# Hybrid diffusion step: the merge takes over h's buffers and runs beside the last gate projections, the MLP's first part stays in the merge's PSUM set, and the modulation sums are spread anew

## The chip, the cores and the metric

The kernel runs on one core of a Trainium2 chip. The metric is device time in microseconds (us) of one execution, as a median over runs. The profile is one execution, taken by the hardware profiler.

## The reference

Two token sets (512 noisy latent tokens, 128 context tokens, so T = 640 rows of width 1024) go through two layers with the same weights. Cut to what matters here:

```python
mod = silu(c) @ w_mod[l] + b_mod[l]                  # 6 vectors of 1024, for c and for c_ctx
sh1, sc1, g1, sh2, sc2, g2 = split(mod, 6)           # vectors 0, 1, 2, 3, 4, 5
h = rmsnorm(x, g_pre_mix) * (1 + sc1) + sh1
z = h @ w_in                                         # q, k, v of mixers A, B, C and 3072 gate columns
oa, ob, oc = three attention mixers
m = (sigmoid(ga) * (oa @ w_oa) + sigmoid(gb) * (ob @ w_ob) + sigmoid(gc) * (oc @ w_oc))
x = x + g1 * rmsnorm(m @ w_out, g_post_mix)
h = rmsnorm(x, g_pre_mlp) * (1 + sc2) + sh2
x = x + g2 * rmsnorm(square(relu(h @ w_mlp1)) @ w_mlp2, g_post_mlp)
```

Everything is float32. The kernel forms each product from high and low halves of its operands, three matmuls per tile.

## The kernel before

The Python code does not issue instructions at once. It records them with the tiles that they read and write, and a list scheduler (`Recorder`) then puts all of them into one order per engine. In that order TensorE (PE) takes ready work by its place in the recorded program, and the other engines by how late an operation may be. A tile pool that opens at the place of a closed one lets no instruction of its own be placed before the last instruction of the closed one has been. All DMAs are issued by SP, in order, so one that waits holds back those behind it. Since one function issues every recorded operation, the profile names line 526 for all of them, and rows are told apart by tile names.

A layer l runs through these stages (times of layer 0, of layer 1 in brackets):

- Mixer B (to 280 us; to 1480 us): projections, `b_rope`, then eight heads.
- Mixers A and C (280 to 607 us; 1480 to 1762 us), called AC below. Attention is a chain over PE, ScalarE (ACT), VectorE (DVE) and GpSimd (POOL): products into `sps`, softmax into `pt`, transposes into `tps`, products into `ops`.
- Fillers run beside both. `gate_gen` computes the 24 gate blocks in 48 half steps (24 matmuls into `gps`, a tanh on ACT, a DMA of `th` to DRAM) and needs h, which lives in `hh` and `hl`. `mod_gen` computes the modulation vectors. One vector has two halves, and each half has four steps that load 512 KB of `w_mod` and add them into `macc0` on DVE and `macc1` on POOL (7 additions per half), and one step with small matmuls into `mps`. The rates say how many filler steps go with a step of attention. Inside attention `mod_gen` loads into `wr`, a ring of three buffers that all weights share.
- The merge (617 to 700 us; 1782 to 1870 us): `merge` loads the mixers' outputs back from DRAM (12 loads `orw`), splits them into `oh` and `ol`, and multiplies into `sps`, in the order of mixers 1 (B), 0 (A), 2 (C); the gates come back as `tg`. The result m goes to `mh` and `ml`.
- `wout` (products `fps`, then norm and transposes `nps`), then `mlp1_first`, the first 512 columns of the MLP in two parts: 384 tokens, then 256.
- `up` (the rest of the MLP's first product) and `down` (`mlp2_block`), with modulation sums as fillers that have a ring `mr` of their own.

Before the change, gates and sums end first, then the pools of the fillers and of h close, and the merge's pools open in their place. PSUM has eight banks. The merge and `wout` use the set big=2 (two tiles of two banks), pt=2, o=1, fill=1, and `mlp1_first` opens the set ring=6, pt=2.

Of the kernel before, what the change touches and what calls it, by code (L numbers as in the profile page):

```python
# [11 lines left out]
F32 = mybir.dt.float32  # L12
F32R = mybir.dt.float32r
# [4 lines left out]
P = 128  # L18
D = 1024
KC = 8  # L20
DEPTH = 2
NT = 5
T = 640
# [11 lines left out]
GATE_RATE_B = 0.03  # L35
MOD_RATE = 0.2
GATES_FIRST = 2
# [9 lines left out]
ACT_BUFS = 10  # L47
UP_RATE = (0.7, 0.5)
DOWN_RATE = (1.6, 0.5)

# [479 lines left out]
class Step:  # L530
# [1380 lines left out]
    def run(self):  # L1911
        nc, tc, I, O = self.nc, self.tc, self.I, self.O
        with ExitStack() as ctx:
# [14 lines left out]
            self.hh = hp.tile([P, KC, T], F32R, name="hh")  # L1928
            self.hl = hp.tile([P, KC, T], F32R, name="hl")
            with pool("n0") as np_:  # L1930
                self.first_norm(np_, xin)
# [4 lines left out]
            for l in range(DEPTH):  # L1936
                self.fine = False
                stack2 = ExitStack()
                fpool = stack2.enter_context(pool(f"fill{l}", "right"))
                mods = [self.mod_gen(fpool, 0, (2, 3, 4, 5))] if l == 0 else []  # L1940
                gl = [self.gate_gen(fpool, l)]
                fills = gl + mods

                with pool(f"b{l}") as bp:
# [13 lines left out]
                    with pool(f"bh{l}") as bh, self.banks(f"psb{l}", big=2, ring=4, alias={"pt": "ring", "fill": "ring", "o": "ring"}):  # L1958
                        self.NP = P_BUFS_B
                        hs = self.b_heads(bh, l)  # L1960
                        self.drive(hs[0][0], (fills, 1))
                        self.drive(self.zip(hs[0][1], hs[1][0]), (gl, GATE_RATE_B), (mods, MOD_RATE))
                        for h in range(8):
                            steps = [hs[h][2]]
                            if h < 7:
                                steps.append(hs[h + 1][1])
                            if h < 6:
                                steps.append(hs[h + 2][0])
                            self.drive(self.zip(*steps), (gl, GATE_RATE_B if h < 7 else 1), (mods, MOD_RATE))

                self.fine = True
                with pool(f"ac{l}") as ap, self.banks(f"psac{l}", big=2, ring=3, o=1, alias={"pt": "ring", "fill": "ring"}):
# [17 lines left out]
                    self.finish(*gl, *mods)  # L1990
                stack2.close()
                stack.close()
                pstack = ExitStack()
                pstack.enter_context(self.banks(f"ps{l + 1}", big=2, pt=2, o=1, fill=1))

                stack = ExitStack()
                with pool(f"mm{l}", sides[l % 2]) as mmp, pool(f"wx{l}", sides[l % 2]) as wx:
                    mh = mmp.tile([P, KC, T], F32R, name="mh")
                    ml = mmp.tile([P, KC, T], F32R, name="ml")
                    us = {}  # L2000
# [4 lines left out]

                    with pool(f"m{l}") as mp:
                        mg = self.merge(mp, l, mh, ml)
                        self.finish(itertools.islice(mg, 33))
                        load(0, wx)
                        self.finish(mg)  # L2010
                    hside = sides[1 - l % 2]
                    hp = stack.enter_context(pool(f"h2{l}", hside))
                    self.h2h = hp.tile([P, KC, T], F32R, name="h2h")
                    self.h2l = hp.tile([P, KC, T], F32R, name="h2l")
                    hstack = ExitStack()
                    self.hfull = hstack.enter_context(pool(f"hf{l}", hside)).tile([P, KC, T], F32, name="hfull")
                    with pool(f"w{l}") as wp:
# [23 lines left out]
                with pool(f"up{l}", side) as mp:  # L2041
                    t = self.sums(mp)
                    self.finish(self.mlp1_first(mp, "r", 3, l, us, slice(FIRST_TOKENS, T)))
                    self.hfull = None
                    hstack.close()
                    modp = hstack.enter_context(pool(f"md{l}", hside))
                    mods = [self.mod_gen(modp, 1, (5,), 2)] if last else [self.mod_gen(modp, l + 1, range(5), 2)]
                    kept = {"pool": kstack.enter_context(pool(f"kept{l}", hside))}
                    halfs = self.halfs()

                    def up():
                        for n in range(4, 32, 2):
                            self.mlp1_pair(mp, l, n, t, halfs, kept if n >= 32 - KEPT else None)
                            yield

                    self.drive(up(), (mods, UP_RATE[l]))
                with pool(f"dn{l}", side) as mp:
# [13 lines left out]
                    with pool(f"end{l}", hside) as ep:  # L2071
# [14 lines left out]
                hstack.close()  # L2086
                self.hh, self.hl = self.h2h, self.h2l
# [62 lines left out]
```

## Time and profile before

| | before |
|---|---|
| runs | 2389.28, 2395.51, 2398.93 us (median 2395.51) |
| profiled execution | 2388.71 us |
| its span, first to last instruction | 2386.9 us |
| PE busy | 2296.2 us (96%) |
| DVE busy | 1703.2 us (71%) |
| ACT busy | 1294.2 us (54%) |
| POOL busy | 767.6 us (32%) |
| mean granted PE clock | 0.988 |

The span is shorter than the execution by 1.8 us, which lie before the first and after the last instruction. A granted clock of 1.00 is 2.4 GHz and 0.50 is 1.2 GHz. In a stretch with a mean clock of 0.79, a share of 0.21 of the stretch is lost as against the full clock.

### The profile page before, as it was taken

The numbers are of one execution on the slowest core, as the hardware profiler recorded it, in microseconds if no ns is written. First come the engines' busy times: TensorE is split into PE (matmuls) and PEld (weight loads), VectorE is DVE, ScalarE is ACT, GpSimd is POOL, SyncE is SP. The second block draws the span as 40 slices with busy tenths as digits, with TensorE's granted clock in tenths as the row PEclk, the third lists the DMA queues.
The fourth block names the chain that finished last, engine by engine and source line by source line (L and its number), as shares of the span: only waits on it lengthen the run. The fifth ranks groups of instructions, "written<-read, shape, count | busy, mean of one in ns | idle before, by whom it ended". The sixth has DMA issues, their size and how long they took to land. (4 is left out here: it accounts for less than half of the span.)

```text
span 2386.9 us, 39558 instructions
## 1 busy us (share of the span) xinstructions
PE 2296.2 (96%) x14303; PEld 2101.0 (88%) x14303; DVE 1703.2 (71%) x3347; ACT 1294.2 (54%) x2996; POOL 767.6 (32%) x671
## 2 busy tenths in 40 slices
PE   8998999999899899999999999999989999999998
PEld 3987999989898899987889989999989988998886
DVE  3689678797574899888865684776756659895444
ACT  4578566666334566654444674655653355664222
POOL 1346233452132366334421121233312315650001
PEclk9999999999899999999999999999999999999999
DMA  7443423333563454576534323222236543546432
GB/s 248 117 141 99 141 76 100 102 108 104 179 198 117 147 164 156 172 239 218 175 111 106 74 65 92 64 63 77 74 101 199 172 135 132 172 140 208 129 116 82
DMA packets 252451, 317.10 MB, mean 133 GB/s; under 512 B 37328, under 2 KB 169696, under 8 KB 251744
## 3 DMA queue, kind: packets, MB, share of 16 engines
q1 hardware_dynamic: 252256, 314.58, 42.0%
q8 instruction: 113, 1.85, 0.3%
q14 instruction: 82, 0.67, 0.1%
HBM read 251.84 MB, written 57.44 MB: 130 GB/s over the span
## 5 line engine op out<-in xcount | busy, mean ns | idle before, releaser
L526 DVE TENSOR_TENSOR wl<-wr,wh 128x256 fp32r<-128x256 f32 (+5 forms) x768 | 380.4, 543 | 151.5 <-ACT wh L526 147.0
L526 ACT ACTIVATE wh<-wr 128x256 fp32r<-128x256 f32 (+5 forms) x768 | 276.1, 421 | 206.0 <-PE lps L526 122.5
L526 POOL TENSOR_SCALAR pt<-pt,rc 128x640 f32<-128x640 f32 (+1 forms) x192 | 168.8, 887 | 361.9 <-DVE rc L526 310.4
L526 PE MATMUL lps<-wh,ah 128*128 128x512 f32 x640 | 254.1, 397 | 0.0
L526 PE MATMUL lps<-wl,ah 128*128 128x512 f32 x640 | 253.1, 395 | 0.0
L526 PE MATMUL lps<-wh,al 128*128 128x512 f32 x640 | 253.0, 395 | 0.0
L526 POOL TENSOR_TENSOR rs<-ss,mhalf 128x1 f32<-128x1 f32 x60 | 38.2, 637 | 453.9 <-DVE ss L526 453.7
L526 POOL TENSOR_TENSOR macc<-macc,mr 128x512 f32<-128x512 f32 x84 | 126.2, 1503 | 171.8 <-ACT mr L526 155.5
L526 DVE TENSOR_TENSOR pl<-tps,ph 128x512 fp32r<-128x512 f32 (+2 forms) x240 | 147.5, 630 | 32.5 <-ACT ph L526 30.2
L526 ACT ACTIVATE pt<-sps,nm 128x640 f32<-128x640 f32 (+2 forms) x192 | 141.7, 740 | 44.6 <-DVE nm L526 38.8
L526 PE MATMUL sps<-h2h,wl 128*128 128x320 f32 (+2 forms) x464 | 145.3, 313 | 12.1 <-DVE wl L526 12.1
L526 PE MATMUL sps<-h2h,wh 128*128 128x320 f32 (+2 forms) x464 | 145.7, 314 | 6.2 <-DVE f L526 6.2
L526 ACT ACTIVATE ph<-tps 128x512 fp32r<-128x512 f32 (+2 forms) x240 | 129.6, 555 | 30.2 <-PE tps L526 26.7
L526 PEld LDWEIGHTS lps<-wl,ah 128*128 128x128 f32 x640 | 120.7, 189 | 28.4 <-issue 0.7
L526 PEld LDWEIGHTS lps<-wh,ah 128*128 128x128 f32 x640 | 120.7, 189 | 28.0 <-issue 0.5
L526 PEld LDWEIGHTS lps<-wh,al 128*128 128x128 f32 x640 | 120.6, 188 | 27.6 <-issue 0.2
L526 PE MATMUL sps<-h2l,wh 128*128 128x320 f32 (+2 forms) x464 | 144.7, 312 | 0.0
L526 PE MATMUL tps<-ident,pt 128*128 128x128 f32 x896 | 140.3, 275 | 4.1 <-POOL pt L526 3.0
L526 PE MATMUL sps<-oh,wh 128*128 128x320 f32 x384 | 122.1, 321 | 16.2 <-ACT oh L526 16.2
L526 POOL TENSOR_TENSOR s<-wq 128x512 f32<-128x512 f32 x56 | 90.2, 1611 | 134.6 <-DMA wq<-in_w_mlp 102.3
L526 DVE TENSOR_TENSOR wl<-s,wh 128x512 fp32r<-128x512 f32 x112 | 129.0, 1165 | 4.0 <-ACT wh L526 3.9
L526 PE MATMUL sps<-ol,wh 128*128 128x320 f32 x384 | 122.8, 321 | 0.0
(335 smaller groups left out, 7341.7 us busy)
## 6 DMA issues: line engine op xcount, KB each, us to landing
wr<-in_w_in SPq DMA_DIRECT2D x72, 512.0 KB, 3.8
wr<-in_w_mlp SPq DMA_DIRECT2D x72, 512.0 KB, 4.1
wq<-in_w_mlp SPq DMA_DIRECT2D x56, 512.0 KB, 4.7
mr<-in_w_mod SPq DMA_DIRECT2D x48, 512.0 KB, 4.5
ar<-a SPq DMA_DIRECT2D x56, 320.0 KB, 4.9
wr<-in_w_mod SPq DMA_DIRECT2D x32, 512.0 KB, 3.7
th<-th SPq DMA_DIRECT2D x96, 160.0 KB, 2.0
tg<-th SPq DMA_DIRECT2D x48, 320.0 KB, 3.0
```

Source lines behind the costliest of these rows:

```text
L526: getattr(getattr(self.nc, o.eng), o.name)(*args, **kw)
```

## The change

- Layer l's last four gate steps (`GATES_LAST`) are taken out of attention's list and driven beside the first steps of `merge`. For that the filler pool and h's pool stay open, and `mh` and `ml` take the ring places of `hh` and `hl` (for layer 1 of `h2h` and `h2l`) instead of a pool of their own. Layer 1's filler pool moves to the left side.
- The merge's PSUM set becomes big=2, pt=2, fill=2, and stays open through the first part of `mlp1_first`.
- The vectors' sums move: before, layer 0's attention computes vectors 2 to 5 of layer 0, layer 0's MLP vectors 0 to 4 of layer 1, and layer 1's MLP vector 5 of layer 1. Now attention of each layer computes that layer's vectors 2 to 4 with rate 0 in mixer B's heads and 0.3 in AC, layer 0's MLP computes vector 5 of layer 0 and vectors 0 and 1 of layer 1, and layer 1's MLP vector 5 as before. The MLP's rates fall from 0.7 and 1.6 to 0.5 and 1.0.

```diff
-MOD_RATE = 0.2
+MOD_RATE = 0.3
+MOD_RATE_B = 0.0
+GATES_LAST = 4
...
-UP_RATE = (0.7, 0.5)
-DOWN_RATE = (1.6, 0.5)
+UP_RATE = (0.5, 0.5)
+DOWN_RATE = (1.0, 0.5)
...
-                fpool = stack2.enter_context(pool(f"fill{l}", "right"))
-                mods = [self.mod_gen(fpool, 0, (2, 3, 4, 5))] if l == 0 else []
-                gl = [self.gate_gen(fpool, l)]
+                fpool = stack2.enter_context(pool(f"fill{l}", sides[1 - l % 2]))
+                mods = [self.mod_gen(fpool, l, (2, 3, 4))]
+                gates_left = self.gate_gen(fpool, l)
+                gl = [itertools.islice(gates_left, 48 - GATES_LAST)]
...
-                            self.drive(self.zip(*steps), (gl, GATE_RATE_B if h < 7 else 1), (mods, MOD_RATE))
+                            self.drive(self.zip(*steps), (gl, GATE_RATE_B if h < 7 else 1), (mods, MOD_RATE_B))
...
-                stack2.close()
-                stack.close()
                 pstack = ExitStack()
-                pstack.enter_context(self.banks(f"ps{l + 1}", big=2, pt=2, o=1, fill=1))
+                pstack.enter_context(self.banks(f"ps{l + 1}", big=2, pt=2, fill=2))
...
-                with pool(f"mm{l}", sides[l % 2]) as mmp, pool(f"wx{l}", sides[l % 2]) as wx:
-                    mh = mmp.tile([P, KC, T], F32R, name="mh")
-                    ml = mmp.tile([P, KC, T], F32R, name="ml")
+                hstack, stack = stack, ExitStack()
+                with hstack, pool(f"wx{l}", sides[l % 2]) as wx:
...
+                        mh = hp.tile([P, KC, T], F32R, name="mh", tag=htags[0])
+                        ml = hp.tile([P, KC, T], F32R, name="ml", tag=htags[1])
                         mg = self.merge(mp, l, mh, ml)
-                        self.finish(itertools.islice(mg, 33))
+                        self.drive(itertools.islice(mg, 33), ([gates_left], 1))
                         load(0, wx)
                         self.finish(mg)
+                    stack2.close()
...
-                        pstack.close()
-                        pstack = ExitStack()
-                        pstack.enter_context(self.banks(f"psm{l}", ring=6, pt=2, alias={"fill": "ring", "o": "ring"}))
                         self.finish(self.mlp1_first(wp, "xr", 2, l, us, slice(0, FIRST_TOKENS), turns))
+                    pstack.close()
+                    pstack = ExitStack()
+                    pstack.enter_context(self.banks(f"psm{l}", ring=6, pt=2, alias={"fill": "ring", "o": "ring"}))
...
-                    mods = [self.mod_gen(modp, 1, (5,), 2)] if last else [self.mod_gen(modp, l + 1, range(5), 2)]
+                    mods = [self.mod_gen(modp, l, (5,), 2)]
+                    if not last:
+                        mods = [itertools.chain(*mods, self.mod_gen(modp, l + 1, (0, 1), 2))]
```

What this does to the order of instructions is shown at three places. The first is SP's queue where layer 0's merge begins; `th_0_22` and `th_0_23` are outputs of the last gates, `o_0_2` is the attention output that is written last, and `orw` reads the outputs back. Before:

```order
L526 DMA th_0_22_8093<-th_8089 128x320
L526 DMA o_0_2_7039<-oraw_7705 128x640
L526 DMA th_0_22_8093<-th_8127 128x320
L526 DMA wr_8156<-in_w_oc 128x4x256
L526 DMA th_0_23_8173<-th_8167 128x320
L526 DMA th_0_23_8173<-th_8193 128x320
L526 DMA orw_8217<-o_0_1_2015 128x640
L526 DMA orw_8222<-o_0_1_2015 128x640
```

And the same place in the changed kernel:

```order
L528 DMA o_0_2_6933<-oraw_7612 128x640
L528 DMA orw_7992<-o_0_1_1951 128x640
L528 DMA orw_7997<-o_0_1_1951 128x640
L528 DMA orw_8001<-o_0_1_1951 128x640
L528 DMA tg_8006<-th_0_8_4208 128x640
L528 DMA tg_8011<-th_0_9_4498 128x640
L528 DMA tg_8015<-th_0_0_982 128x640
L528 DMA tg_8020<-th_0_1_1088 128x640
L528 DMA th_0_22_8036<-th_8030 128x320
L528 DMA orw_8059<-o_0_1_1951 128x640
```

The first three `orw` loads stood behind the outputs of all gates; now they stand right behind the last attention output, ahead of the last four gates' outputs, of which the first three stand between later loads.

The second place is PE at the same point. `gps` rows are gate products, `sps` rows the merge's. Before:

```order
L526 MATMUL gps_8164<-hh_346,wh_7615 128x320
L526 MATMUL gps_8164<-hl_351,wh_7615 128x320
L526 MATMUL gps_8164<-hh_346,wl_7622 128x320
L526 MATMUL sps_8240<-oh1_8238,wh_7812 128x320
L526 MATMUL sps_8244<-oh1_8238,wh_7812 128x320
L526 MATMUL sps_8240<-ol1_8242,wh_7812 128x320
```

And in the changed kernel:

```order
L528 MATMUL gps_8027<-hl_343,wh_7522 128x320
L528 MATMUL gps_8027<-hh_338,wl_7529 128x320
L528 MATMUL sps_8064<-oh1_8043,wh_7318 128x320
L528 MATMUL sps_8064<-ol1_8050,wh_7318 128x320
L528 MATMUL sps_8064<-oh1_8043,wl_7417 128x320
L528 MATMUL sps_8064<-oh1_8043,wh_7318 128x320
L528 MATMUL gps_8072<-hh_338,wh_8066 128x320
L528 MATMUL gps_8072<-hl_343,wh_8066 128x320
L528 MATMUL sps_8064<-ol1_8050,wh_7318 128x320
```

Before, PE had three gate steps between the last `ops` product of attention and the merge, and no gate after. Now it has two, and the last two are mixed into the merge's first products. In layer 1 it was 140 rows of gate products (5.8 steps) behind the last `ops`, and is 236 rows (9.8 steps), of which 48 are mixed into the merge. Four steps moved there from `b_rope`, where layer 1's sums now take every second filler place.

The third place is SP in layer 1's AC part, with the weights' loads into the shared ring `wr`. Before, they are projection and gate weights (`in_w_in`) alone:

```order
L526 DMA wr_18413<-in_w_in 128x8x128
L526 DMA th_1_10_18248<-th_18435 128x320
L526 DMA wr_18545<-in_w_in 128x8x128
L526 DMA th_1_11_18729<-th_18722 128x320
L526 DMA out_new_c_v<-pz_18836 128x128
L526 DMA wr_18883<-in_w_in 128x8x128
```

In the changed kernel the sums' weights (`in_w_mod`) stand among them:

```order
L528 DMA wr_18676<-in_w_in 128x8x128
L528 DMA o_1_0_17986<-oraw_17702 128x640
L528 DMA wr_18777<-in_w_mod 128x2x512
L528 DMA wr_18910<-in_w_in 128x8x128
L528 DMA th_1_10_18972<-th_18964 128x320
L528 DMA wr_19046<-in_w_mod 128x2x512
L528 DMA wr_19121<-in_w_mod 128x2x512
```

Layer 1's AC part had no sums; now about every second load of the ring is one of theirs.

## Rows read from the trace of the kernel before

**Rows 1.** The page: busy time of each engine.

```profile
PE 2296.2 (96%) x14303; PEld 2101.0 (88%) x14303; DVE 1703.2 (71%) x3347; ACT 1294.2 (54%) x2996; POOL 767.6 (32%) x671
```

**Rows 2.** Stretches: start:end, length, busy of each engine (count), PEclk, DMA share.

```profile
617.00:649.00 32.00, 22.89 (x121) 21.61 (x120) 18.15 (x25) 13.19 (x25) 4.16 (x2) 0.79 0.69 233
1782.00:1813.00 31.00, 23.85 (x121) 21.64 (x121) 16.95 (x25) 13.08 (x25) 3.81 (x2) 0.78 0.74 241
120.00:280.00 160.00, 147.97 (x975) 133.59 (x974) 134.11 (x267) 115.88 (x264) 73.33 (x67) 0.99 0.45 132
1320.00:1480.00 160.00, 154.60 (x1070) 143.84 (x1068) 109.36 (x248) 103.17 (x252) 32.18 (x44) 1.00 0.27 75
280.00:600.00 320.00, 311.65 (x2302) 299.77 (x2300) 253.43 (x623) 203.48 (x523) 125.54 (x130) 1.00 0.33 97
1480.00:1760.00 280.00, 276.14 (x2028) 264.49 (x2029) 208.38 (x544) 176.74 (x466) 84.21 (x103) 1.00 0.24 69
1000.00:1240.00 240.00, 234.83 (x1072) 191.47 (x1070) 195.25 (x289) 122.35 (x256) 94.42 (x68) 0.99 0.57 189
```

**Rows 3.** PE in order of time: start, duration, instruction, idle time before it.

```profile
622.07 0.64 PE L526 MATMUL sps<-oh,wh 128*128 128x320 f32 x1 [4.85 <-ACT oh L526]
777.98 0.41 PE L526 MATMUL sps<-h2h,wh 128*128 128x384 f32 x1 [3.08 <-DVE f L526]
813.76 0.64 PE L526 MATMUL sps<-h2h,wl 128*128 128x320 f32 x1 [6.35 <-DVE wl L526]
1942.47 0.42 PE L526 MATMUL sps<-h2h,wh 128*128 128x384 f32 x1 [3.09 <-DVE f L526]
```

**Rows 4.** SP in order of time, around the start of layer 0's merge.

```profile
608.04 0.32 SPq L526 DMA_DIRECT2D o<-oraw  x1
...
614.24 3.84 SPq L526 DMA_DIRECT2D th<-th  x2
618.17 1.35 SPq L526 DMA_DIRECT2D orw<-o  x3
```

**Rows 5.** ACT in order of time, the splits of the merge's inputs.

```profile
621.28 1.60 ACT L526 ACTIVATE oh<-orw 128x640 fp32r<-128x640 f32 x2 [2.33 <-DMA orw<-o]
...
630.69 2.35 ACT L526 ACTIVATE oh<-orw 128x640 fp32r<-128x640 f32 x3 [6.62 <-DMA orw<-o]
...
644.47 0.74 ACT L526 ACTIVATE oh<-orw 128x640 fp32r<-128x640 f32 x1 [1.04 <-DMA orw<-o]
```

**Rows 6.** Gate products alone, between attention's last product and the merge.

```profile
606.80:617.30 10.50, 10.41 (x72) 10.15 (x70) 0.88 (x3) 1.00 0.38 128
```

**Rows 7.** Two slices of 40 us, columns as in rows 2.

```profile
160.00:200.00 40.00, 36.45 (x215) 30.75 (x215) 38.65 (x71) 32.00 (x74) 20.66 (x19) 0.96 0.39 110
760.00:800.00 40.00, 36.92 (x216) 34.22 (x215) 24.42 (x52) 22.98 (x61) 2.58 (x4) 1.00 0.36 120
```

**Rows 8.** DVE and PE in order of time, between layer 0's wout and up.

```profile
782.31 0.76 DVE L526 TENSOR_SCALAR f<-xr,rs 128x1024 f32<-128x1024 f32 x1
...
790.55 0.71 PE L526 MATMUL nps<-ident,f 128*128 128x128 f32 x5
```

**Rows 9.** Instructions on macc alone (the modulation sums), columns as in rows 2.

```profile
120.00:280.00 160.00, 7.49 (x40) 5.20 (x40) 31.88 (x38) 2.90 (x4) 38.66 (x26) 0.99 0.45 132
280.00:600.00 320.00, 7.49 (x40) 5.21 (x40) 29.32 (x34) 2.17 (x3) 32.30 (x23) 1.00 0.33 97
1000.00:1240.00 240.00, 15.34 (x104) 13.07 (x104) 57.24 (x70) 5.07 (x7) 81.57 (x56) 0.99 0.57 189
```

**Rows 10.** Who PE waited for in 1000 to 1240 us: total, times, longest.

```profile
PE mps L526 <- DVE macc L526: 2.3, 1, 2.3
```

**Rows 11.** DVE in order of time; POOL adds run from 802.90 us on.

```profile
802.24 0.82 DVE L526 TENSOR_TENSOR t1l<-hfull,t1h 128x640 fp32r<-128x640 f32 x1
802.98 1.92 DVE L526 TENSOR_TENSOR t0l<-hfull,t0h 128x640 fp32r<-128x640 f32 x1
...
802.90 1.31 POOL L526 TENSOR_TENSOR s<-wq 128x512 f32<-128x512 f32 x1 [20.63 <-DMA wq<-in_w_mlp]
```

More of the change, by code (lines that the diff above doesn't have):

```diff
@@ L1929, in run @@
             self.hl = hp.tile([P, KC, T], F32R, name="hl")
+            htags = ("hh", "hl")
             with pool("n0") as np_:
@@ L1961, in run @@
                         self.drive(hs[0][0], (fills, 1))
-                        self.drive(self.zip(hs[0][1], hs[1][0]), (gl, GATE_RATE_B), (mods, MOD_RATE))
+                        self.drive(self.zip(hs[0][1], hs[1][0]), (gl, GATE_RATE_B), (mods, MOD_RATE_B))
                         for h in range(8):
@@ L1990, in run @@
                     self.finish(*gl, *mods)
-                stack2.close()
-                stack.close()
                 pstack = ExitStack()
-                pstack.enter_context(self.banks(f"ps{l + 1}", big=2, pt=2, o=1, fill=1))
-                stack = ExitStack()
-                with pool(f"mm{l}", sides[l % 2]) as mmp, pool(f"wx{l}", sides[l % 2]) as wx:
-                    mh = mmp.tile([P, KC, T], F32R, name="mh")
-                    ml = mmp.tile([P, KC, T], F32R, name="ml")
+                pstack.enter_context(self.banks(f"ps{l + 1}", big=2, pt=2, fill=2))
+                hstack, stack = stack, ExitStack()
+                with hstack, pool(f"wx{l}", sides[l % 2]) as wx:
                     us = {}
@@ L2014, in run @@
                     self.h2l = hp.tile([P, KC, T], F32R, name="h2l")
-                    hstack = ExitStack()
-                    self.hfull = hstack.enter_context(pool(f"hf{l}", hside)).tile([P, KC, T], F32, name="hfull")
+                    htags = ("h2h", "h2l")
+                    fstack = ExitStack()
+                    self.hfull = fstack.enter_context(pool(f"hf{l}", hside)).tile([P, KC, T], F32, name="hfull")
                     with pool(f"w{l}") as wp:
@@ L2044, in run @@
                     self.hfull = None
-                    hstack.close()
-                    modp = hstack.enter_context(pool(f"md{l}", hside))
-                    mods = [self.mod_gen(modp, 1, (5,), 2)] if last else [self.mod_gen(modp, l + 1, range(5), 2)]
+                    fstack.close()
+                    modp = fstack.enter_context(pool(f"md{l}", hside))
+                    mods = [self.mod_gen(modp, l, (5,), 2)]
+                    if not last:
+                        mods = [itertools.chain(*mods, self.mod_gen(modp, l + 1, (0, 1), 2))]
                     kept = {"pool": kstack.enter_context(pool(f"kept{l}", hside))}
@@ L2085, in run @@
                                 turn()
-                hstack.close()
+                fstack.close()
                 self.hh, self.hl = self.h2h, self.h2l
```

## The prediction

> **What bounds the kernel now.** I read the page first: PE is busy for 2296.2 us of a span of 2386.9 us [rows 1], so no change of order can win more than the 90.7 us in which PE stands still and what a lower clock costs on top. The change removes no work. Everything hangs on where PE waits, so I went through PE's idle time in order of time and then through the busy times by stretch. Three places stand out.
>
> At the start of each merge PE is idle for 9.11 of 32 us and for 7.15 of 31 us, and the granted clock falls to a mean of 0.79 and 0.78, which is a part of each stretch at 1.2 instead of 2.4 GHz [rows 2]. The wait's releaser is ACT's split of a merge input [rows 3], but ACT itself waited for the load [rows 5]. The load is late because SP is: it issued the last attention output at 608.04 us, then stood behind two gate outputs, and reached the first `orw` only at 618.17 us [rows 4]. PE's gates had ended at 617.2 us (622.07 less 4.85 [rows 3]). From the first issue to the split of the last input it takes 27.0 us (618.17 to 644.47 and 0.74 more [rows 4, 5]), with PE behind it all the time.
>
> Between `wout` and the MLP, PE waits 3.08 us in layer 0 and 3.09 in layer 1 for DVE's work on the last `fps` tile [rows 3], whose PSUM banks the set ring=6 takes over.
>
> In mixer B of layer 0, with sums, PE is idle for 12.03 of 160 us; in layer 1, without sums, for 5.40 of 160. In AC it is 8.35 of 320 us with sums (layer 0) and 3.86 of 280 without (layer 1) [rows 2].
>
> **The merges.** Each loses its idle time and its clock: layer 0 9.11 + 0.21 x 32 = 15.8 us, layer 1 7.15 + 0.22 x 31 = 14.0 us [rows 2]. How much comes back, on the time scale of before: the loads of layer 0 now stand right behind the attention output, at about 608.4 instead of 618.2 us. A gate step of 24 products takes 24/72 x 10.41 = 3.5 us [rows 6]. Two steps remain ahead of the merge instead of three, so PE asks for the first input at 617.2 - 3.5 = 613.7 us. The first split can start at 608.4 + 3.1 = 611.5 (621.28 less 618.17 [rows 4, 5]). The fourth input is split 12.5 us after the first issue plus about 1.5 us for both halves, so at 622.4; by the order PE asks for it after some 53 further products of 0.145 us, at 621.4. Inputs 9 to 12 must be there when mixer C's products begin, 48 gate and 96 merge products later, at 634.6; the last is ready at 608.4 + 27.0 + 0.8 = 636.2, but is asked for a few products late. SP now waits for gate outputs between these loads, which end before the inputs behind them are needed. In attention's last products one gate step no longer covers the last split; I put 1 us on that. Together about 3 us remain, in pieces of 1 us, and 12.8 us are won. In layer 1 three whole gate steps, two mixed ones and four steps of mixers B and A, 31 us, stand between the first loads and mixer C's products, against 28 us of loading: 0.5 us remain, 13.5 are won. The clock should stay up: after the wait of 3.08 us the slice from 760 to 800 us shows 1.00 [rows 7]. `mh` waits for the last gates' reads of `hh`, but is first written after six merge steps (21 us), behind the gates. Layer 1's filler pool on the other side I cost at nothing: its first tiles come when the MLP's last rows are done, as before.
>
> **The MLP's first part.** It needs tokens 0 to 383 alone, which are ready, and with fill=2 its banks are free. Does the wait only move? The norm's input f is done at 783.1 us and its transposes run at 790.55 [rows 8], so three earlier microseconds of PE are followed by the chain behind them. The next wait, 6.35 us for a weight split on DVE [rows 3], hangs on that chain and stays as long as it is. I take the whole 3.08 + 3.09 = 6.2 us; least is nothing, if DVE is late by as much more there.
>
> **The sums.** 26 of layer 0's POOL additions ran in mixer B, 23 in AC [rows 9]. A vector has 14, so three vectors have 42. By the order about 7 come in `b_rope`'s stretch and 35 in AC, in each layer. Mixer B of layer 0 should then look like that of layer 1: 12.03 - 5.40 = 6.6 us, and the clock of 0.96 in one slice of 40 us [rows 7] gives 1.6 more, 8.2 in all; I take 7.5. In `down` of layer 0 there are fewer sums: 2.3 us of PE's wait for `macc` [rows 10] and 0.01 x 240 = 2.4 us of clock [rows 2] are what could go, 4.7 us; additions fall from 56 [rows 9] to about 32 (42 of three vectors, less some 10 at the rate of `up`), so I take half, 2.5.
>
> AC pays. Layer 0 gets 12 additions more, layer 1 all 35. From below: 3.9 us more idle (8.35 less 3.86 x 320/280) for 23 additions are 0.17 us each, 47 x 0.17 = 8 us. I take a price by load. DVE's share and PE's idle share are 74% and 1.4% in AC without sums, 79% and 2.6% with, 68% and 3.4% in mixer B without, 84% and 7.5% with [rows 2]. Both pairs give about 0.25 points of idle for a point of DVE. An addition brings 29.32/23 = 1.27 us of DVE [rows 9]. Layer 0's AC goes to (253.43 + 12 x 1.27)/320 = 84%, five points, 4.0 us. Layer 1's goes to (208.38 + 35 x 1.27)/280 = 90%, sixteen points, 11.3 us. Together 15.3 us lost. From above: in the densest slice of mixer B DVE is at 97%, PE loses 8.9% and the clock 4% [rows 7]; less the 1.4% that layer 1's AC has already, 11.5% of 280 us are 32 us, and 40 us with 8 for layer 0.
>
> **A rule that speaks against it.** DVE's split with two inputs in SBUF takes 0.82 us, and 1.92 us beside POOL's additions [rows 11], 1.1 us more. By that row 35 additions could stretch DVE's other work in layer 1's AC by 38 us, to 292 us of 280. The Trainium skill (SBUF — State Buffer, section "Who interferes with whom") says that such a DVE instruction and a GpSimd one that reads SBUF exclude each other for a whole instruction. The trace agrees in kind: DVE's time more than doubles. AC of layer 0, with 23 additions, doesn't show DVE full at 253 of 320 us, so I leave this in the rivals.
>
> **Sum.** 12.8 + 13.5 + 6.2 + 7.5 + 2.5 - 15.3 = 27.2 us. The profiled execution took 2388.7 us (span 2386.9 and 1.8 around it), so its twin should take 2361.5. The median of the runs lies 6.8 us above the profiled one; I forecast 2368 us for it.
>
> **Rivals.**
> - *The load still sets the merge's start.* The outputs of the last gates stand between the loads on SP, so a late tanh delays the inputs behind it. For it: one wait of SP behind `th` is what made the loads late before. Against: three loads go ahead now, and PE has work. If half of both merge losses stays, 13 us less is won: 2381 us.
> - *DVE becomes the bound in layer 1's AC.* For it: 90% by my sum, and the 1.92 us above. Against: AC's PE idles least of all stretches. DVE's 292 us at 97% are 301 us, 21 us more instead of 11; with 4% of the clock and 6 us in layer 0's AC the gain falls to about 2 us: 2393 us.
> - *Slower: the weights' ring.* In AC, sums hold the three `wr` buffers until POOL has added, and now take every second place in layer 1. A projection or gate weight that comes late makes PE wait, as the 6.35 us for `wl` show [rows 3]. Against: with 23 additions in layer 0's AC, PE is idle for 8.35 us in all. The kernel ends slower by over 0.5% (12 us) once this costs 39 us more than I count, which is over six such waits. With eight, 51 us, it takes 2419 us.
> - *The sums are nearly free* (0.17 us each or less) and all covers hold: 2354 us or less.
>
> **Chances.** My forecast 0.58 (own range 2357 to 2379), sums nearly free 0.10, load still late 0.13, DVE the bound 0.13, weights' ring 0.06. About 0.5%, 12 us, is what a measurement of this kernel can tell from no change. The forecast, the free sums and most of the late load lie beyond it: faster 0.80, within it 0.14 (DVE as the bound, and a little of the late load), slower 0.06. The range reaches from 2350, all the covers at their best, to 2386 us, so that DVE as the bound and the ring stay outside.
>
> **What would show it.** Right: no PE wait above 2 us and a clock of 1.00 at both merges; no wait at the MLP's first product, the later wait for `wl` about 6 us as before; mixer B of layer 0 idle for about 5.5 of 160 us; AC of layer 1 idle for about 15 us with DVE near 90%. Wrong: waits of PE for `wl`, `pl` or `pt` in AC that add up to over 30 us, a wait above 4 us for `oh` with a clock of 0.50 behind it, or a wait for `wl` before `up` that grew by 3 us.

## The result, and the profile after

The changed kernel takes 2359.06 us, the median of four runs (2356.36 to 2359.53), against 2395.16 us of the kernel before on the same chip; the ratio is 0.9849, with a 95% interval of 0.9828 to 0.9871. Forecast were 2368 us, so it is 9 us faster than that and within the range. The profiled execution took 2356.36 us.

The page: busy time of each engine, which answers to [rows 1], and the granted clock in 40 slices. PE has 9.6 us less of busy time and stands still for 68.0 instead of 90.7 us (span less busy time).

```profile
span 2354.6 us, 39546 instructions
PE 2286.6 (97%) x14303; PEld 2089.6 (89%) x14303; DVE 1700.6 (72%) x3351; ACT 1289.2 (55%) x3000; POOL 763.2 (32%) x671
PEclk9999999999999999999999999999999999999999
```

Busy times by stretch, columns as in [rows 2]; the borders are those of the stages in this kernel: heads of mixer B, layer 0; mixers A and C ("AC"), layer 0; its start of the merge; `down` of layer 0; heads of layer 1; AC of layer 1; its start of the merge.

```profile
122.90:262.00 139.10, 133.27 (x902) 122.51 (x901) 100.93 (x218) 93.96 (x226) 30.33 (x40) 1.00 0.28 77
262.00:594.90 332.90, 322.94 (x2362) 307.51 (x2361) 280.88 (x650) 213.06 (x543) 142.22 (x142) 1.00 0.36 105
594.90:630.00 35.10, 33.83 (x222) 32.26 (x221) 21.10 (x34) 15.40 (x33) 3.25 (x2) 1.00 0.82 273
964.00:1196.00 232.00, 231.96 (x1049) 190.03 (x1048) 146.97 (x252) 102.59 (x223) 53.05 (x38) 1.00 0.52 167
1278.90:1417.50 138.60, 133.29 (x901) 122.55 (x899) 100.42 (x217) 93.92 (x226) 30.34 (x40) 1.00 0.28 77
1417.50:1731.30 313.80, 303.35 (x2223) 287.00 (x2222) 265.78 (x628) 208.84 (x525) 139.84 (x142) 1.00 0.36 104
1731.30:1790.00 58.70, 57.69 (x392) 57.22 (x392) 26.73 (x49) 23.00 (x56) 6.30 (x4) 1.00 0.64 209
```

The two merges start with 1.3 and 1.0 us of idle time and a clock of 1.00, where [rows 2] had 0.79 and 0.78. AC of layer 1 pays: PE is idle for 10.4 of 313.8 us there, DVE is busy for 85%. Before, between the same two stage borders, it was idle for 4.0 of 294.8 us and DVE was busy for 73%:

```profile
1467.10:1761.90 294.80, 290.76 (x2151) 278.75 (x2150) 216.03 (x572) 183.62 (x485) 86.05 (x107) 1.00 0.24 68
```

SP and ACT in order of time around the start of layer 0's merge, as in [rows 4, 5]. The first `orw` goes out 0.4 us after the last attention output, not 10.1; a tanh output (`th`) stands between the loads now. From the first issue to the split of the last input it takes 29.9 us (596.73 to 626.60), 2.8 more than before. PE now waits little for it: 0.57 us for the low half of that last input (`ol`, in the rows behind the next ones).

```profile
596.31 0.32 SPq L528 DMA_DIRECT2D o<-oraw  x1
596.73 1.44 SPq L528 DMA_DIRECT2D orw<-o  x3
598.21 2.96 SPq L528 DMA_DIRECT2D tg<-th  x4
601.26 0.48 SPq L528 DMA_DIRECT2D th<-th  x1
...
601.22 0.74 ACT L528 ACTIVATE oh<-orw 128x640 fp32r<-128x640 f32 x1 [2.30 <-DMA orw<-o]
...
625.88 0.72 ACT L528 ACTIVATE oh<-orw 128x640 fp32r<-128x640 f32 x1
```

In layer 1 the loads do not go right behind the last attention output. They go 16.5 us after it (20.1 before the change), behind five gate outputs instead of six; but PE, which had ended its gates 0.9 us before the first load went out, now has 9.6 us of whole gate steps left at that time.

```profile
1732.68 0.32 SPq L528 DMA_DIRECT2D o<-oraw  x1
...
1748.85 0.32 SPq L528 DMA_DIRECT2D th<-th  x1
1749.22 1.39 SPq L528 DMA_DIRECT2D orw<-o  x3
```

PE in order of time, with the idle time ahead of each instruction, as in [rows 3]: the longest wait at each merge, the wait before `up` in each layer, and a new one where layer 1 begins.

```profile
628.70 0.41 PE L528 MATMUL sps<-ol,wh 128*128 128x320 f32 x1 [0.57 <-DVE ol L528]
788.89 0.51 PE L528 MATMUL sps<-h2h,wl 128*128 128x320 f32 x1 [4.67 <-DVE wl L528]
1218.86 0.40 PE L528 MATMUL lps<-wh,h2h 128*128 128x288 f32 x1 [2.71 <-DVE h2h L528]
1784.15 0.41 PE L528 MATMUL sps<-ol,wh 128*128 128x320 f32 x1 [1.01 <-DVE ol L528]
1944.67 0.64 PE L528 MATMUL sps<-h2h,wl 128*128 128x320 f32 x1 [5.12 <-DVE wl L528]
```

Where the time went, by stage. "Idle" is the sum of the gaps between PE's instructions in the stage. "Clock" is half of the time in which the granted clock stood at 1.2 GHz outside these gaps, since a product takes nearly twice as long there (in the kernel before, 0.27 us from one 128x320 product to the next, against 0.146 at the full clock), so it is a little too high. For `up` and ahead of the heads the two are added up.

| stage | idle + clock before | after | won |
|---|---|---|---|
| merge, layer 0 | 9.1 + 5.0 | 1.3 + 0 | 12.8 |
| merge, layer 1 | 7.1 + 5.6 | 1.0 + 0 | 11.7 |
| MLP's first part, both layers | 3.1 and 3.1 | 0 and 0 | 6.2 |
| `up`, both layers | 8.4 and 8.1 | 6.4 and 7.6 | 2.5 |
| heads of mixer B, layer 0 | 12.0 + 1.6 | 5.8 + 0 | 7.8 |
| `down`, layer 0 | 3.5 + 1.7 | 0 + 0 | 5.2 |
| AC, layer 0 | 8.4 + 0 | 10.0 + 0 | -1.6 |
| AC, layer 1 | 4.0 + 0 | 10.4 + 0 | -6.4 |
| turn to layer 1 | 3.8 + 0 | 4.4 + 1.7 | -2.3 |
| ahead of the heads, layer 0 | 12.3 | 13.2 | -0.9 |

These give 35.0 us. The span is shorter by 32.3: PE's other busy time, at full clock, is 2.7 us longer. Each stage is read from one execution, and the small rows are not firm. In the change and six runs below with the same AC of layer 0, PE is idle there for 9.1 to 11.4 us and loses 0 to 3.4 us of clock. Ahead of the heads, idle time and clock make 10.5 to 14.9 us in kernels that do the same work there.

### The profile page after: what moved, and what is told of

Its sections match the earlier page's. It is cut to its first block, busy times and chain, and to the rows that moved or that the text cites. A ratio compares the mean times of both kernels' runs of the same rounds, so it can differ in the third digit from the quotient of the medians.

```text
span 2354.6 us, 39546 instructions
## 1 busy us (share of the span) xinstructions
PE 2286.6 (97%) x14303; PEld 2089.6 (89%) x14303; DVE 1700.6 (72%) x3351; ACT 1289.2 (55%) x3000; POOL 763.2 (32%) x671
## 5 line engine op out<-in xcount | busy, mean ns | idle before, releaser
L528 DVE TENSOR_TENSOR wl<-wr,wh 128x256 fp32r<-128x256 f32 (+5 forms) x772 | 370.5, 527 | 145.0 <-ACT wh L528 143.6
L528 ACT ACTIVATE ph<-tps 128x512 fp32r<-128x512 f32 (+2 forms) x240 | 130.4, 555 | 33.0 <-PE tps L528 29.9
L528 POOL TENSOR_TENSOR macc<-macc,wr 128x512 f32<-128x512 f32 x84 | 118.3, 1409 | 57.2 <-ACT wr L528 44.4
L528 POOL TENSOR_TENSOR macc<-macc,mr 128x512 f32<-128x512 f32 x56 | 87.7, 1566 | 140.5 <-ACT mr L528 92.9
L528 DVE TENSOR_TENSOR wl<-s,wh 128x512 fp32r<-128x512 f32 x112 | 123.3, 1114 | 3.4 <-ACT wh L528 2.2
L528 PE MATMUL gps<-hh,wh 128*128 128x320 f32 x384 | 120.1, 313 | 2.2 <-ACT th L528 1.7
```

Of the source, the lines that this page charges most:

```text
L528: getattr(getattr(self.nc, o.eng), o.name)(*args, **kw)
```

## The experiments

All times are medians; ratios are to the kernel before, run beside each kernel.

**The change without its new spread of the sums.**

```diff
-MOD_RATE = 0.3
-MOD_RATE_B = 0.0
+MOD_RATE = 0.2
+MOD_RATE_B = 0.2
...
-UP_RATE = (0.5, 0.5)
-DOWN_RATE = (1.0, 0.5)
+UP_RATE = (0.7, 0.5)
+DOWN_RATE = (1.6, 0.5)
...
-                mods = [self.mod_gen(fpool, l, (2, 3, 4))]
+                mods = [self.mod_gen(fpool, 0, (2, 3, 4, 5))] if l == 0 else []
...
-                    mods = [self.mod_gen(modp, l, (5,), 2)]
-                    if not last:
-                        mods = [itertools.chain(*mods, self.mod_gen(modp, l + 1, (0, 1), 2))]
+                    mods = [self.mod_gen(modp, 1, (5,), 2)] if last else [self.mod_gen(modp, l + 1, range(5), 2)]
```

> The changed kernel with the modulation sums spread as before (layer 0's vectors 2 to 5 in its attention at 0.2, five vectors of layer 1 in layer 0's MLP at 0.7 and 1.6, vector 5 in layer 1's). Theory A, from the stages of the two traces: the new spread wins 7.9 us in mixer B of layer 0 and 5.2 in down, and costs 1.6 and 6.4 us in the two AC parts, so this kernel takes about 5 us more than the changed one, some 2364 us, with PE idle and slowed for about 13 us in mixer B of layer 0 and for about 4 us in layer 1's AC. Theory B, the sizes of the prediction: AC pays 15.3 us and the rest wins 10, so this kernel takes 5 us less, some 2354 us. Theory C: the sums matter only through the merge's start; no difference from 2359 us beyond 2 us.

Measured: 2360.22 us, ratio 0.9876 (0.9860 to 0.9891), which doesn't stand apart from the kernel after. Both merges keep their gain (1.4 and 1.0 us idle, no loss of clock). The heads of layer 0 (13.8 + 3.2 us) and `down` (3.4 + 5.0) have their losses of before again, AC of layer 1 is back at 3.9. So Theory A's stages come, but its 5 us do not show in the median. The profiled execution is the slowest of the four (2366.85 us), so its clock losses may be more than usual.

**The new spread alone**, on the kernel before: the lines above the other way round, and the vectors of each layer where the change has them.

```diff
-                mods = [self.mod_gen(fpool, 0, (2, 3, 4, 5))] if l == 0 else []
+                mods = [self.mod_gen(fpool, l, (2, 3, 4))]
```

> The kernel before with nothing changed but the spread of the sums. Theory A: about 5 us less than before, some 2390 us; both merges still wait 9 and 7 us for the loads with the clock at 0.50 in part of it, and the MLP's first product waits 3.1 us twice. Theory B: about 5 us more than before, 2400 us. Theory C (the parts of the change help each other): nothing alone, 2395 us, and more than 5 us lost where it is taken out of the changed kernel.

Measured: 2389.62 us, ratio 0.9998 (0.9988 to 1.0008): nothing. The heads win 7.8 us and `down` 5.2; AC of layer 0 loses 2.0 + 1.7, AC of layer 1 5.7 + 1.7, and the turn to layer 1 0.6 + 1.7. Against 13.0 won stand 13.4 lost. The waits of 3.09 us in each layer at the MLP's first product are there, as before. So what the whole change wins is not in the sums.

**All gates in the attention again**, everything else changed; and the same with the fillers' pool closed ahead of the merge (the second and third line), as before the change.

```diff
-GATES_LAST = 4
+GATES_LAST = 0
...
+                stack2.close()
                 pstack = ExitStack()
...
-                    stack2.close()
```

> The changed kernel with all 48 gate steps ahead of the merge, pools still open as in the change. By the order the first loads of the merge now stand behind all gate outputs but the last one, so they come only one gate step (3.5 us) earlier than in the kernel before. Theory A (the load's place behind the gate outputs made the stall): most of it returns, PE waits 4 to 7 us in each merge with the clock at 0.50 behind it, 16 to 22 us are lost, 2375 to 2381 us. Theory D (the open pools alone let the loads go ahead): PE waits less than 2 us, 2359 to 2363 us.

> As the one with all gates ahead of the merge, and the fillers' pool closed before the merge as in the kernel before, so that the merge's loads stand behind all gate outputs. h's buffers still go to m. Theory A: the stalls of the kernel before return in full (PE idle for 9 and 7 us, clock at 0.50 for about 14 us in each layer), 25 to 27 us more than the changed kernel, about 2385 us, and 5 to 8 us more than with the pool open. Theory D: all of the gain of the merge hangs on this pool, so 2385 us here against 2359 to 2363 with it open.

Measured: 2373.10 us, ratio 0.9929 (0.9915 to 0.9942), and 2380.02 us, ratio 0.9960 (0.9947 to 0.9974). SP's issues show what each part does: first with the gates early, then with the pool closed as well.

```profile
597.67 0.32 SPq L528 DMA_DIRECT2D o<-oraw  x1
...
603.88 0.32 SPq L528 DMA_DIRECT2D th<-th  x1
604.29 1.35 SPq L528 DMA_DIRECT2D orw<-o  x3
...
609.60 0.51 SPq L528 DMA_DIRECT2D th<-th  x1
```

```profile
601.02 0.32 SPq L528 DMA_DIRECT2D o<-oraw  x1
...
607.23 3.84 SPq L528 DMA_DIRECT2D th<-th  x2
611.16 1.35 SPq L528 DMA_DIRECT2D orw<-o  x3
```

| kernel | last `o` to first `orw`, layers 0 and 1 | lead of the first `orw`, layers 0 and 1 | merge of layer 0, idle + clock | layer 1 |
|---|---|---|---|---|
| before | 10.1 and 20.1 us | -1.0 and -0.9 us | 9.1 + 5.0 | 7.1 + 5.6 |
| gates early, pool closed | 10.1 and 34.2 | -1.0 and -1.0 | 7.4 + 4.4 | 8.0 + 4.5 |
| gates early | 6.6 and 30.6 | 2.6 and 2.6 | 5.6 + 3.3 | 5.9 + 4.6 |
| the change | 0.4 and 16.5 | 5.2 and 9.6 | 1.3 + 0 | 1.0 + 0 |

"Lead" is the time from the issue of the first `orw` to the end of PE's last gate product ahead of the merge.

In layer 0 three gate outputs follow the last `o`. With the pool closed the loads stand behind all three, with it open behind two, with four steps kept back behind none. In layer 1 they stand behind ten, nine and five, so the distance from the last `o` does not order the losses there. The lead does, in both layers: what counts is how much of PE's gate work is left when the loads go out. In the change two more gate steps besides are mixed into the merge. The open pool is worth 2.9 and 2.0 us, the four late steps 7.6 and 9.5.

**The kernel after, once more**, as the measure for three kernels on the same chip: the PSUM set opened early, the sums computed twice, and three vectors moved.

> The kernel after once more, unchanged, as the measure for the kernels beside it. It should stand at 2357 to 2362 us, with a ratio of 0.983 to 0.988 to the kernel before.

Measured: 2360.49 us, ratio 0.9866 (0.9846 to 0.9886). PE is idle for 9.1 and 10.1 us in the two ACs.

**The MLP's PSUM set opened ahead of its first part again.**

```diff
+                        pstack.close()
+                        pstack = ExitStack()
+                        pstack.enter_context(self.banks(f"psm{l}", ring=6, ...))
                         self.finish(self.mlp1_first(wp, "xr", 2, l, us, slice(0, FIRST_TOKENS), turns))
-                    pstack.close()
-                    pstack = ExitStack()
-                    pstack.enter_context(self.banks(f"psm{l}", ring=6, ...))
```

> The kernel after, with the PSUM set of six rings opened ahead of the MLP's first part, as before the change. Theory A (the early products win their whole wait): PE again waits about 3.1 us at the MLP's first product in each layer, the wait for the split of a weight before the up products stays at 4.7 and 5.1 us, and the kernel is 5 to 6 us slower than the kernel after, near 2365 us. Theory B (the wait only moves): the wait of 3.1 us returns, but the one before the up products shrinks by 2 to 3 us in each layer, and the time changes by less than 1.5 us.

Measured: 2360.98 us, ratio 0.9866 (0.9849 to 0.9883), the time of the kernel after. Both theories fell. PE goes from the last transposes to the MLP's first product without a wait, although the set is opened early; only the wait before `up` is longer, 6.35 and 5.77 us. In layer 0 that is 1.7 us more than in both profiles of the kernel after (4.67); in layer 1 these two differ themselves (5.12 and 4.07), so it is 0.6 to 1.7 us.

```profile
754.76 1.03 PE L528 MATMUL nps<-ident,f 128*128 128x128 f32 x8
755.55 0.42 PE L528 MATMUL sps<-h2h,wh 128*128 128x384 f32 x1
...
791.35 0.63 PE L528 MATMUL sps<-h2h,wl 128*128 128x320 f32 x1 [6.35 <-DVE wl L528]
```

**The same, and no gate steps beside the merge:** the edit above, and

```diff
-GATES_LAST = 4
+GATES_LAST = 0
```

> The kernel with the PSUM set of six rings opened early again, and besides with no gate steps beside the merge (all of them end in the attention). The run before this one showed no wait at the MLP's first product although the set was opened early. Theory A: that wait is decided by which banks the new set's first tiles take; with gates beside the merge their two banks come first in the merge's set and are long free, without them the last output product's banks come first. Then PE waits about 3.1 us at the MLP's first product in each layer, and both merges start late as without late gates, near 2376 to 2380 us. Theory B: the wait went with something else (m in h's buffers, fewer tiles of the set); then no wait above 0.5 us is seen there.

Measured: 2383.99 us, one run. The wait is back in both layers (3.09 and 3.10 us), as Theory A has it.

```profile
765.75 0.42 PE L528 MATMUL sps<-h2h,wh 128*128 128x384 f32 x1 [3.09 <-DVE f L528]
...
800.46 0.63 PE L528 MATMUL sps<-h2h,wl 128*128 128x320 f32 x1 [5.28 <-DVE wl L528]
```

Gates early with the first part in the merge's set have no such wait, nor have late gates with the set opened early; only with both undone is it there. Either part of the change removes it. That the reason is the order of the banks (the gates' two are the first that the merge's set gives out, and the next set's first tiles take them) is Theory A's, read from the code; no run showed bank numbers. Nor does the wait only move: the one before `up` is 5.3 and 6.8 us here against 4.7 and 5.1 with the gates early alone.

**Layer 1's three vectors computed twice in its attention**, at twice the rate; the second time is redundant.

```diff
-                mods = [self.mod_gen(fpool, l, (2, 3, 4))]
+                mods = [itertools.chain(*[self.mod_gen(fpool, l, (2, 3, 4)) for i in range(1 + l)])]
...
-... (mods, MOD_RATE))
+... (mods, MOD_RATE * (1 + l)))
```

> The kernel after, with three vectors' sums of layer 1 computed twice in its attention, at twice the rate: some 35 additions of GpSimd more in the second stretch of mixers A and C, with the weights that they load; the extra work is redundant. Theory A (each addition costs PE about 0.18 to 0.26 us, at any load): 6 to 9 us more than the kernel after, 2365 to 2368 us, PE idle for 15 to 19 us in that stretch. Theory B (VectorE becomes the bound: it is busy for 266 of 314 us there, and 35 additions more are 50 us): VectorE at over 97%, 20 us or more on top, 2380 us or later. Theory C (by the prediction's price for load, 0.25 points of idle for a point of VectorE, 16 points to the full): 11 to 14 us more, 2371 to 2374 us.

Measured: 2430.50 us, ratio 1.0157 (1.0140 to 1.0174), 70 us over the kernel after. Busy times in AC of layer 1, and in one slice of 40 us:

```profile
1422.70:1804.50 381.80, 340.58 (x2294) 312.74 (x2293) 337.94 (x692) 240.53 (x573) 206.28 (x184) 0.94 0.42 124
1470.00:1510.00 40.00, 34.01 (x231) 30.82 (x230) 39.07 (x74) 26.04 (x62) 28.61 (x23) 0.97 0.52 161
```

Instructions on `macc` alone (POOL's additions are the count in the fifth pair), here and then in the kernel after:

```profile
1422.70:1804.50 381.80, 25.80 (x144) 19.57 (x144) 98.99 (x104) 7.96 (x11) 112.97 (x77) 0.94 0.42 124
```

```profile
1417.50:1731.30 313.80, 11.22 (x72) 8.92 (x72) 39.64 (x48) 3.63 (x5) 49.25 (x35) 1.00 0.36 104
```

Who PE waited for in that stretch of the doubled kernel: total us, times, longest.

```profile
PE mps L528 <- DVE macc L528: 7.9, 5, 2.4
PE qps L528 <- DVE qst L528: 5.0, 3, 3.4
...
PE ops L528 <- DVE pl L528: 3.8, 5, 1.5
```

Cut into nine slices of 40 us from 1422 us on, the stretch has DVE at 97 to 99% in three (the slice shown has 39.07 us); over the whole of it DVE is at 89%. Of the waits, 27.8 us were ended by DVE, 8.1 by ACT and 4.5 by POOL; the staged queries (`qst`) now wait behind the sums, in the longest case for 3.4 us. The stretch is 68.3 us longer than in the rerun of the kernel after: 31.1 idle, 20.4 clock, 11.8 for the sums' own products at full clock (25.80 less 11.22, less 2.8 that the clock has counted), 5.0 unexplained. For 42 additions more, idle and clock make 1.23 us each. Theories A (0.18 to 0.26 us at any load) and C fell. The time is Theory B's, and most waits end with DVE as it says; its DVE share of over 97% is seen only in slices.

**Layer 1's vectors in the MLP of layer 0:** all three, one, or two of them.

```diff
-                mods = [self.mod_gen(fpool, l, (2, 3, 4))]
+                mods = [self.mod_gen(fpool, l, ((2, 3, 4), (3, 4))[l])]
...
-                        mods = [itertools.chain(*mods, self.mod_gen(modp, l + 1, (0, 1), 2))]
+                        mods = [itertools.chain(*mods, self.mod_gen(modp, l + 1, range(3), 2))]
```

This is the one with one vector; two and three move the border, and the rates with it.

> The kernel after, with three vectors of layer 1 back in the MLP of layer 0 (its rates 0.7 and 1.9) and none in the attention of layer 1; layer 0's attention keeps its three. Theory A (a price by place): the second stretch of mixers A and C wins back 6 to 9 us (PE idle for about 4 us), the down products of layer 0 lose 5 us or less, and the kernel is 1 to 4 us faster than the kernel after, 2355 to 2358 us. Theory B (the additions cost the same anywhere): the same time within 1 us. Theory C (the MLP at a rate of 1.9 is where additions are dear): PE waits for the sums' banks in the down products, 10 us or more lost there, 2362 us or later.

> The kernel after, with one vector of layer 1 moved from its attention to the MLP of layer 0 (two stay; the rate in layer 1's attention is 0.67 of layer 0's, those of up and down 0.55 and 1.3). Theory A (the price of an addition rises with the load, so that the middle is best): the second stretch of mixers A and C of layer 1 is idle for 6 to 8 us instead of 10, down of layer 0 for 1 us or less, and the kernel is 2 to 5 us faster than the kernel after, 2355 to 2358 us. Theory B (the price is the same in either place): the same time as the kernel after within 1.5 us.

> The kernel after, with two vectors of layer 1 in the MLP of layer 0 (one stays in its attention, at a third of layer 0's rate; up and down at 0.7 and 1.6, as before the change). Theory A (the price rises with the load): the second stretch of mixers A and C of layer 1 is idle for 4 to 6 us, down of layer 0 for 3 to 4 us as before the change, with up to 5 us of clock, and the kernel is 1 to 5 us faster than the kernel after, 2355 to 2359 us. Theory B: the same time as the kernel after within 1.5 us.

Measured: three 2357.25 us, ratio 0.9847 (0.9825 to 0.9868); one 2352.59, 0.9829 (0.9805 to 0.9853); two 2356.47, 0.9839 (0.9814 to 0.9864). All lie below the rerun of the kernel after (0.9866), but the intervals overlap, so none is shown to be faster. One and two were run on another chip than the rerun. The stages are steadier than the times: AC of layer 1 with one vector moved, then its `macc` instructions,

```profile
1425.00:1730.50 305.50, 299.08 (x2215) 286.01 (x2214) 245.30 (x604) 199.29 (x509) 116.14 (x128) 1.00 0.29 86
1425.00:1730.50 305.50, 7.43 (x64) 7.50 (x64) 21.88 (x24) 2.15 (x3) 28.25 (x21) 1.00 0.29 86
```

and all five kernels together, by the additions that run in that stretch:

| AC of layer 1 | additions | DVE busy | idle + clock | `down` of layer 0: additions, idle + clock |
|---|---|---|---|---|
| three in the MLP | 0 | 73% | 4.3 + 0 | 70, 7.4 + 1.7 |
| two | 7 | 75% | 4.5 + 0 | 56, 0.3 + 1.7 |
| one | 21 | 80% | 6.4 + 0 | 42, 0.05 + 0 |
| the change (rerun) | 35 | 85% | 10.1 + 0 | 28, 0.04 + 0 |
| computed twice | 77 | 89% | 41.2 + 20.4 | 28, 0.04 + 0 |

From row to row an addition costs 0.03, 0.14, 0.26 and 1.23 us. Only the last step is firm: in seven executions with 35 additions the idle time runs from 9.1 to 10.4 us and the clock's loss from 0 to 1.7, so the first three prices are not told apart; from 0 to 35 additions the mean is 0.17. In `down` the last 14 look dear as well (7.1 us, 0.5 each), but 56 additions at the same rates lost 5.2 us before the change and 8.4 with the old spread, so that step isn't firm either. One vector moved wins 3.7 us of idle time in AC and loses nothing in `down`: the stages that Theory A forecast for it. With two, `down` lost less than Theory A said; with three, AC won 5.8 us and `down` lost 9.0, more than Theory A's 5 and less than Theory C's 10.

**Some of each layer's additions back in the heads of mixer B**, on top of one vector moved.

```diff
-MOD_RATE = 0.3
-MOD_RATE_B = 0.0
+MOD_RATE = 0.23
+MOD_RATE_B = 0.1
```

> The kernel with one vector of layer 1 in the MLP, and besides some 7 of the additions of each layer's attention moved out of the second stretch (mixers A and C) into the heads of mixer B, where the change had taken them all out (rate 0.1 there, 0.23 behind it). Theory A (the price of an addition rises with the load of its stretch, so thin spreading is best): the second stretch is idle for 7 to 9 us instead of 10 to 11 in layer 0 and for 4.5 to 6 instead of 6.4 in layer 1, the heads of mixer B grow by 1 us of idle time or less in each layer, and the time is 1 to 4 us below that of one vector alone, 2349 to 2352 us. Theory B (mixer B is dear at any rate: before the change 26 additions cost it 6.3 us, 0.24 each): the heads grow by 1.5 to 2 us in each layer, and the time is the same or up to 2 us more.

Measured: 2358.33 us, ratio 0.9848 (0.9824 to 0.9872), no better than one vector alone. The heads of layer 0 with their 8 additions, all instructions and then those on `macc`:

```profile
123.34:272.28 148.94, 137.65 (x909) 124.29 (x907) 112.97 (x237) 100.11 (x236) 42.59 (x48) 1.00 0.37 103
123.34:272.28 148.94, 3.76 (x8) 1.51 (x8) 14.22 (x18) 1.42 (x2) 10.75 (x8) 1.00 0.37 103
```

They are idle for 11.3 us instead of 5.9, of which one wait of 2.2 us is for a load of `qd`; layer 1's heads, with as many, for 5.7 instead of 5.3. AC wins 2.2 us of idle time in layer 0 and loses 3.4 of clock; in layer 1 it is idle for 0.8 us more, 7.2 us with 13 additions against 6.4 with 21, which is within what equal work differs by. Theory A fails in layer 0, where it is worse even than Theory B said, and isn't borne out in layer 1.

## Why the prediction was right, and where not

- **The merges** were forecast at 12.8 and 13.5 us; they won 12.8 and 11.7. The mechanism is the one told: SP stood behind the gates' outputs (three in layer 0, at 610.67, 614.24 and 617.76 us, not the two of [rows 4]), and the experiment with the gates early brings most of the loss back with the lead of the loads. Layer 1 came out as its count of steps said, nearly three whole ones left on PE at the first load, though SP still issues five gate outputs first. The first figure is right by two errors. The clock's mean of 0.79 was taken over the whole of the 32 us, idle time included, so the loss before was counted as 15.8 where it was 14.1; and 3 us were left where 1.3 remained. In layer 1 it was 12.7, not 14.0. The longest wait left in either merge (0.57 and 1.01 us) is for the low half of the last input, which the prediction had as the late one.
- **The MLP's first part**: forecast 6.2, won 6.2. The step named two reasons, what the part needs and free banks with fill=2. The runs show that the early placing isn't needed for it while gates run beside the merge. The other bound, that the wait only moves, fell: the wait before `up`, forecast as unchanged, shrank as well (2.5 us for `up` with its clock). With the set opened early it is back at 6.35 us in layer 0, so there it comes from the early placing; in layer 1 the difference is hardly more than that between two executions.
- **Mixer B of layer 0**: forecast 7.5, won 7.8. **`down`**: forecast 2.5, won 5.2, all that [rows 2, 10] had to give. The half that was taken was too careful: 42 additions there still cost nothing; 56 cost 2.0 us in one kernel, 5.2 before the change and 8.4 with the old spread (in its slowest execution).
- **AC** is the term that was mis-sized: forecast 15.3 lost, measured 8.0 (1.6 and 6.4). The count was right, 35 additions in each layer. The failing step is "both pairs give about 0.25 points of idle for a point of DVE": DVE went to 85% in layer 1 rather than 90%, since the working divided by the old length of a stretch that grows with the sums' products and waits; and a point cost 0.17 points of idle there (1.95 for 11.4) and 0.08 in layer 0 (0.43 for 5.7). The lower bound, 0.17 us an addition, gives 8 us and was right in this execution. Over seven executions with 35 additions in each AC, idle time and clock together cost 6.1 to 12.5 us more than before; the high ones lose clock, for which the working had no term. All lie under 15.3. A loss of the size of the upper bound comes further on: 42 additions more cost 51.5 us.
- **Not in the sum**: the turn to layer 1 lost 2.3 us; the spread alone shows the same 2.3, so it is the sums' doing. Ahead of the heads 0.9 us, which is within what equal work differs by from one execution to the next, and 2.7 us of PE's other busy time (3.6 with the spread alone).

Taken together the sums come out at nothing: 7.8 + 5.2 - 8.0 - 2.3 - 2.7 = 0.0, and the spread alone changes nothing either (0.9998). The whole gain is the merges, the MLP's first part and `up`. On the span 32.3 us were won against 27.2 forecast. That the total came this near is in part luck: AC, `down`, `up` and mixer B came out better by 12.8 us, while the merges fell short by 1.8 and 5.9 us were lost in places that had no term. That makes 5.1 of the 9 us by which the median was missed; the other 4 are the profiled execution's place among the runs: 6.8 us below the median before, 2.7 after.

Of the rivals, "the load still sets the merge's start" is ruled out by the waits of at most 0.57 and 1.01 us at the two merges. "DVE becomes the bound in layer 1's AC" did not come about with 35 additions; with 77 most of PE's waits end with DVE. The rule that spoke against the forecast gave 38 us more of DVE's other work in that stretch. DVE's busy time rose there from 216.03 to 265.78 us, of which 39.64 are on `macc`, so its other work grew by about 10 us. DVE's mean for a weight's split over the whole stretch, before, and for a sum's step and a split in the kernel after and in the doubled one:

```profile
L526 DVE TENSOR_TENSOR wl<-wr,wh 128x256 fp32r<-128x256 f32 x96 | 40.6, 469 | 2.3 <-ACT wh L526 1.7 <-issue 0.2
```

```profile
L528 DVE TENSOR_TENSOR wl<-wr,wh 128x256 fp32r<-128x256 f32 x96 | 43.7, 492 | 2.1 <-ACT wh L528 2.0
...
L528 DVE SCALAR_TENSOR_TENSOR macc<-wr,scT,macc 128x512 f32<-128x512 f32 x35 | 31.7, 904 | 0.2
```

```profile
L528 DVE SCALAR_TENSOR_TENSOR macc<-wr,scT,macc 128x512 f32<-128x512 f32 x77 | 82.0, 1065 | 0.3
L528 DVE TENSOR_TENSOR wl<-wr,wh 128x256 fp32r<-128x256 f32 x96 | 47.7, 535 | 0.9 <-ACT wh L528 0.8
```

In these three kernels each piece takes longer with more of POOL's additions, but most of DVE's 72 us more in the doubled kernel are the sums' own work (98.99 less 39.64 on `macc`). The Trainium skill (SBUF — State Buffer, section "Who interferes with whom") has it that a DVE instruction with two inputs in SBUF and a GpSimd one that reads SBUF contend for a shared read interface. The rows agree in direction; they don't separate it from other reasons. "The weights' ring" did not happen: PE never waits for `wl` in the change's AC of layer 1, and for 4.1 us in the doubled one. Nor were the sums nearly free in AC; they were free only in balance.

## What to carry to other kernels

SP issued in order here, so the merge's loads stood behind the stores ahead of them: look at what stands in such a queue ahead of a stage's first load, and keep work that needs neither for the time that the loads take. What counted was how much of that work was left on PE when the first load went out. Price filler by the load of the place that takes it: in layer 1's AC the first 35 additions cost 0.17 us each, the next 42 cost 1.23. One execution of a stage told differences of 1 to 2 us badly; equal work in one of the ACs differed by that much. When a wait is gone, undo the suspected parts one by one and then together; here two parts covered the same 3 us, and each alone looked worth nearly nothing.

## What the runs showed of the hardware that was not expected

- Short waits did not always cost clock: with 10.0 and 10.4 us of idle time in pieces of under 2 us, both ACs kept a mean of 1.00 in the kernel after. That is not sure to hold: in the kernel with three vectors moved, AC of layer 0, idle for 10.2 us in pieces of under 2 us as well, lost 1.7 us of clock. With 41.2 us, in pieces of up to 3.4 us, it fell to 0.94 in layer 1 with the sums computed twice, which cost another 20.4 us, half as much as the waits themselves.
- The same 96 DVE splits of a weight in layer 1's AC took 469 ns on the mean with none of POOL's additions beside them, 462 with 21, 492 with 35 and 535 with 77.
